# Attention outputs as features by queries, two heads to a product, divided by spread reciprocals

## The chip, the cores and the metric

The kernel runs on one core of one Trainium2 chip. TensorE multiplies, VectorE and ScalarE work on elements, GpSimd does a few small things, and SyncE issues the transfers; each works through its own list of instructions in order and waits on semaphores for the others. The metric is the time of one execution on the device in microseconds, as the median of several runs.

## The reference

A trunk of two layers, each a half-step SwiGLU block, a token mixer and another half-step SwiGLU block, on 256 tokens of 1024 features. Every sub-layer is entered through an RMS norm with an adaLN scale and shift and left through an adaLN gate, which are products of the conditioning vector with weights. The first layer's mixer is multi-head latent attention, the second's a Mamba-2 scan (SSD). The change is in the attention, whose core is:

```
def one_block(args):                       # a block of 128 queries, 2 of them
    q_blk, i = args
    s = jnp.einsum('bhqd,bhkd->bhqk', q_blk, kt) * scale      # 16 heads of 96
    s = jnp.where(k_pos[None, :] <= q_pos[:, None], s, -jnp.inf)
    p = jax.nn.softmax(s, axis=-1).astype(vt.dtype)
    return jnp.einsum('bhqk,bhkd->bhqd', p, vt)               # values of 64
...
return o.reshape(Bn, S, MLA_HEADS * V_HEAD) @ w_o
```

Everything is float32. The large products are made of three products of two rounded parts each (a high part and a residue, `split_pair`, `split_act`, `mm3`); the scores and the products with the values are plain float32.

## The kernel before

The features lie on the partitions, the 256 tokens on the free axis. `run` goes through six sub-layers; `mla` (from L811) is the second. Weights come in pieces of 1 MB through five buffers; each piece is split by ScalarE (L206, the high part) and VectorE (L207, the residue `wlo`). The adaLN products are done on VectorE in halves of 128x1024 (L237, `ada_half`), which the program calls wherever there seemed to be room, and which any later sub-layer needs.

The attention goes head by head in turns (`turn`, L1075). In turn t the 16 heads stand at different steps: `scores(t)` on TensorE, queries on the partitions; `softmax(t - 1)`, two maxima on VectorE (L1015, L1016) and two exponentials on ScalarE (L1020), which also leave the sum of a row in `den`; `probs_t(t - 2)`, three transposes of the probabilities; `probs_evac(t - 3)`, their copy to SBUF, by VectorE for three heads of four; `values(t - 4)`. There the transposed probabilities are the stationary side and the 64 columns of a head's values stream, so that a bank holds four heads (a quad) as queries by features. For each quad `o_evac` takes reciprocals of `den` and multiplies (L1053, L1055), `o_t` transposes the result back to features by queries with four transposes, and `o_split` splits it for the output projection. Between the turns the projections of the next quads' queries run. The last turns are hooks of `down`, between products of the output projection (`mwo`).

The order on each engine is not that of the code: the framework's scheduler sets it when the program is built, from priorities and costs of its own, and only instructions that are pinned (`keep_in_program_order`) keep their place. The adaLN halves, the weight splits and the attention are not pinned, so an edit of one moves the others.

A product that resembles the new one is in the SSD scan (`ymm`, L1304): a stationary of 64 columns for each of two heads, into the two halves of the partitions of a bank.

Of the kernel before, what the change touches and what calls it, by code (L numbers as in the profile page):

```python
# [8 lines left out]
F32R = mybir.dt.float32r  # L9
# [3 lines left out]
ALU = mybir.AluOpType  # L13
# [51 lines left out]
class Trunk:  # L65
# [745 lines left out]
    def mla(self, s):  # L811
# [182 lines left out]
        SC, PB, PTs, O, DEN, OT, ON, OB = {}, {}, {}, {}, {}, [], {}, {}  # L994
# [29 lines left out]
        def probs_t(h):  # L1024
            P = SC.pop(h)
            pp = PB[h] = self.bank()
            for b in range(3):
                self.transpose(out=pp[:, b * 128:(b + 1) * 128], in_=P[:, b * 128:(b + 1) * 128],
                                    identity=self.ident)
# [8 lines left out]
        def values(h):  # L1038
            quad, hh = divmod(h, 4)
            half, h8 = divmod(h, 8)  # L1040
            if hh == 0:
                O[quad] = self.bank()
            PT = PTs.pop(h)
            hc = slice(h8 * 64, (h8 + 1) * 64)
            o0 = O[quad][:, hh * 64:(hh + 1) * 64]
            o1 = O[quad][:, 256 + hh * 64:256 + (hh + 1) * 64]
            self.matmul(o1, PT[:, 0:128], V[0][half][:, hc], start=True, stop=False)
            self.matmul(o1, PT[:, 128:256], V[1][half][:, hc], start=False, stop=True)
            self.matmul(o0, PT[:, 256:384], V[0][half][:, hc], start=True, stop=True)

        def o_evac(quad):
            den = DEN.pop(quad)
            nc.vector.reciprocal(out=den, in_=den)  # L1053
            t = ON[quad] = self.slot()
            nc.vector.tensor_tensor(  # L1055
                out=t.rearrange("p (c h d) -> p c h d", c=2, d=64),
                in0=O.pop(quad).rearrange("p (c h d) -> p c h d", c=2, d=64),
                in1=den.rearrange("p c (h o) -> p c h o", o=1).broadcast_to([128, 2, 4, 64]), op=ALU.mult)

        def o_t(quad):  # L1060
            t = ON.pop(quad)
            ps = OB[quad] = self.bank()
            for b in range(2):
                for c in range(2):
                    self.transpose(out=ps[:, b * 256 + c * 128:b * 256 + (c + 1) * 128],
                                        in_=t[:, c * 256 + b * 128:c * 256 + (b + 1) * 128], identity=self.ident)
# [559 lines left out]
```

## Time and profile before

| | |
|---|---|
| median of 3 runs | 1079.45 us (1079.35 to 1080.08) |
| the profiled execution | 1078.63 us |
| its span | 1076.9 us |
| TensorE busy | 1060.8 us, 98% |
| VectorE busy | 872.2 us, 81% |
| ScalarE busy | 617.8 us, 57% |
| chain that ended last | TensorE 92%, DMA 4%, VectorE 3%, ScalarE 1% |

Times of rows are microseconds from the start of the span. PE is TensorE's matmul, DVE is VectorE, ACT is ScalarE. A float32 matmul leaves two records in the trace. Records on one engine overlap a little, since each reaches from its start to its last result: the time that one takes from the engine is the distance to the start of the next, and not its length.

### The profile page before, as it was taken

To read this page: it belongs to the slowest core of one execution; us is meant where nothing else is said; L and a number is where in the kernel's file an instruction comes from. 1 tells how busy PE (TensorE), PEld (TensorE's weight loads), DVE (VectorE), ACT (ScalarE), POOL (GpSimd) and SP (SyncE) were. 2 spreads that over 40 slices of the span, in tenths; PEclk is the share of its full clock that TensorE was granted. 3 is DMA by queue.
4 is the path that set the end of the run, shared out by engine and by line. 5 is a ranking of instruction groups with operands and counts; after the bars stand their busy time and mean duration, and the time that the engine had idled before them with its cause. 6 is when DMAs were issued, how large, how long until landed. Compare 5 with 4: busy or idle time off the path is not lost.

```text
span 1076.9 us, 21729 instructions
## 1 busy us (share of the span) xinstructions
PE 1060.8 (98%) x8814; PEld 1044.1 (97%) x8814; DVE 872.2 (81%) x1551; ACT 617.8 (57%) x1099; POOL 41.3 (4%) x102
## 2 busy tenths in 40 slices
PE   7999999999999999999999999999999999999998
PEld 5999999999999999999999999999999899999998
DVE  5899988889989977767999886599999688756642
ACT  5564544479567444444754544498899567544431
POOL 0000000000010000100000000000211000000000
PEclk9999999999999999999999999999999999999999
DMA  9999998854366988765699987544344354666630
GB/s 353 337 368 342 337 360 321 291 197 148 109 229 221 343 311 312 283 232 202 246 365 346 335 319 250 181 165 157 118 137 170 144 194 161 251 214 214 229 128 21
DMA packets 38264, 259.59 MB, mean 241 GB/s; under 512 B 4370, under 2 KB 5522, under 8 KB 8084
## 3 DMA queue, kind: packets, MB, share of 16 engines
q1 hardware_dynamic: 38164, 258.21, 65.9%
q8 instruction: 69, 1.13, 0.4%
q14 instruction: 31, 0.25, 0.1%
HBM read 257.14 MB, written 1.05 MB: 240 GB/s over the span
## 4 chain that ended last, share of the span: by engine, by line
PE 92%; DMA 4%; DVE 3%; ACT 1%; issue 0%; SPq 0%; ACTq 0%
PE bank L295 91%; DMA raw<-in_adao_dram 3%; PE bank L300 1%; DVE raw L259 1%; DMA raw<-in_xt_dram 0%; DVE wlo L613 0%; ACT sl L808 0%; ACT t L1020 0%; ACT whi L206 0%; DVE sl L1474 0%; DVE ssq L942 0%; ACT t L937 0%; DVE wlo L207 0%; DVE mx L1015 0%; ACT sl L806 0%
## 5 line engine op out<-in xcount | busy, mean ns | idle before, releaser
L295 PE MATMUL bank<-sl,whi 128*128 128x256 f32 (+2 forms) x5360 | 956.2, 282 | 4.9 <-ACT sl L647 3.6
L295 PEld LDWEIGHTS bank<-sl,whi 128*128 128x128 f32 (+1 forms) x5360 | 818.5, 188 | 8.6 <-ACT sl L647 4.6
L295 PE MATMUL bank<-sl,wlo 128*128 128x256 f32 (+2 forms) x2680 | 746.6, 280 | 0.0
L206 ACT CAST whi<-raw 128x1024 fp32r<-128x1024 f32 (+1 forms) x329 | 341.4, 1041 | 339.6 <-PE bank L295 243.8
L295 PEld LDWEIGHTS bank<-sl,wlo 128*128 128x128 f32 (+1 forms) x2680 | 503.6, 188 | 0.2
L207 DVE TENSOR_TENSOR wlo<-raw,whi 128x1024 fp32r<-128x1024 f32 (+1 forms) x329 | 398.1, 1213 | 105.5 <-ACT whi L206 102.0
L237 DVE SCALAR_TENSOR_TENSOR raw<-raw,cb 128x1024 f32<-128x1024 f32 x128 | 154.4, 1218 | 7.6 <-DMA raw<-in_adaw_dram 7.6
L329 ACT CAST sl<-t 128x256 fp32r<-128x256 f32 x125 | 48.6, 403 | 12.2 <-DVE t L521 7.0
L330 DVE TENSOR_TENSOR sl<-t,sl 128x256 fp32r<-128x256 f32 x125 | 51.1, 418 | 1.0 <-ACT sl L329 0.7
L521 DVE TENSOR_TENSOR t<-t,bank 128x256 f32<-128x256 f32 x70 | 28.7, 416 | 15.6 <-PE bank L295 15.6
L460 DVE SCALAR_TENSOR_TENSOR x<-bank,mod,x 128x256 f32<-128x256 f32 x48 | 22.9, 480 | 22.2 <-PE bank L295 21.8
L1159 DVE SCALAR_TENSOR_TENSOR sl<-t,cst,sl 128x256 f32<-128x256 f32 x72 | 34.7, 490 | 0.2
L410 ACT ACTIVATE sl<-x,scol 128x256 fp32r<-128x256 f32 x40 | 20.3, 508 | 23.8 <-DVE x L460 23.7
L520 ACT ACTIVATE t<-bank 128x256 f32<-128x256 f32 x70 | 25.9, 378 | 0.0
L409 POOL CAST sl<-bspl 128x4 fp32r<-128x4 f32 x40 | 12.7, 364 | 319.4 <-PE bank L295 232.6
L259 DVE SCALAR_TENSOR_TENSOR raw<-raw,cb 128x1024 f32<-128x1024 f32 x16 | 19.5, 1222 | 5.9 <-DMA raw<-in_adao_dram 5.8
L295 PE MATMUL bank<-whi,sl 128*128 128x384 f32 (+1 forms) x80 | 24.3, 368 | 0.0
L440 POOL TENSOR_TENSOR rr<-rv,mhalf 128x2 f32<-128x2 f32 x11 | 11.8, 1071 | 304.3 <-DVE rv L436 304.3
L1297 ACT ACTIVATE dec<-sl,nac 128x128 f32<-128x128 f32 x64 | 20.5, 394 | 4.8 <-DVE sl L1286 4.5
L411 DVE SCALAR_TENSOR_TENSOR sl<-x,scol,sl 128x256 fp32r<-128x256 f32 x40 | 19.2, 480 | 4.2 <-ACT sl L410 4.0
L423 ACT ACTIVATE t<-t,mod,scol 128x256 f32<-128x256 f32 x32 | 18.3, 595 | 3.7 <-DVE t L422 3.6
L613 DVE TENSOR_TENSOR wlo<-raw,whi 128x1024 fp32r<-128x1024 f32 (+1 forms) x17 | 19.5, 1156 | 0.0
(215 smaller groups left out, 650.1 us busy)
## 6 DMA issues: line engine op xcount, KB each, us to landing
raw<-in_wgu_dram SPq DMA_DIRECT2D x80, 1024.0 KB, 5.3
raw<-in_adaw_dram SPq DMA_DIRECT2D x64, 1024.0 KB, 6.1
raw<-in_wdn_dram SPq DMA_DIRECT2D x44, 1024.0 KB, 6.2
raw<-in_win_dram SPq DMA_DIRECT2D x19, 1024.0 KB, 4.9
raw<-in_wout_dram SPq DMA_DIRECT2D x8, 1024.0 KB, 4.9
raw<-in_wop_dram SPq DMA_DIRECT2D x6, 1024.0 KB, 6.1
raw<-in_adao_dram SPq DMA_DIRECT2D x6, 1024.0 KB, 8.1
raw<-in_mwo_dram SPq DMA_DIRECT2D x4, 1024.0 KB, 4.9
```

Source lines behind the costliest of these rows:

```text
L206: self.nc.scalar.copy(out=hi, in_=raw)
L207: self.nc.vector.tensor_tensor(out=lo, in0=raw, in1=hi.bitcast(F32), op=ALU.subtract)
L237: nc.vector.scalar_tensor_tensor(out=w, in0=w, scalar=1.0, in1=self.cb, op0=ALU.mult, op1=ALU.mult, accum_out=self.mod[:, q, 2 * u + i:2 * ...
L259: self.order(nc.vector.scalar_tensor_tensor(out=w, in0=w, scalar=1.0, in1=self.cb, op0=ALU.mult, op1=ALU.mult, accum_out=self.mod[:, q, c]))
L295: ins = self.nc.tensor.matmul(*a, **k)
L329: self.nc.scalar.copy(out=hi, in_=src)
L330: self.nc.vector.tensor_tensor(out=lo, in0=src, in1=hi.bitcast(F32), op=ALU.subtract)
L460: nc.vector.scalar_tensor_tensor(out=self.x[m], in0=ps[:, 0:T], scalar=self.mod[:, q, m:m + 1], in1=self.x[m], op0=ALU.mult, op1=ALU.add)
L520: nc.scalar.activation(out=tg, in_=pg[:, 0:T], func=AF.Silu)
L521: nc.vector.tensor_tensor(out=tg, in0=tg, in1=pu[:, 0:T], op=ALU.mult)
L1159: nc.vector.scalar_tensor_tensor(out=dst, in0=u[:, t:t + T], scalar=cw[:, t:t + 1], in1=dst, op0=ALU.mult, op1=ALU.add)
L1297: self.order(nc.scalar.activation(out=t[:, j, 2 * c], in_=q[:, o:o + 128], func=AF.Exp, bias=self.nac[:, c, h:h + 1]))
```

## The change

The products with the values change sides: the values of a head, 64 columns, are the stationary, and the transposed probabilities stream. Two heads (a pair) share a bank, one in each half of the partitions, and the result is features by queries at once. `o_t` goes, and `values` is called for a pair in every second turn. The division now needs each reciprocal on 64 partitions, as a row over the queries: `divisors` takes the reciprocals of a quad's `den` on VectorE and spreads them by eight products with the identity, whose stationary is a column of `den` broadcast to 64; `rows` copies that bank to SBUF on ScalarE; `o_evac` multiplies a pair. The attention needs two turns fewer.

```diff
@@ -991,7 +991,7 @@
         QT[0] = [self.heads_evac(b, None) for b in qb]
         q_evac(1, 1, p1)
 
-        SC, PB, PTs, O, DEN, OT, ON, OB = {}, {}, {}, {}, {}, [], {}, {}
+        SC, PB, PTs, O, DEN, OT, ON, DB = {}, {}, {}, {}, {}, [], {}, {}
 
         def scores(h):
             quad, hh = divmod(h, 4)
@@ -1022,11 +1022,12 @@
             SC[h] = P
 
         def probs_t(h):
+
             P = SC.pop(h)
             pp = PB[h] = self.bank()
             for b in range(3):
-                self.transpose(out=pp[:, b * 128:(b + 1) * 128], in_=P[:, b * 128:(b + 1) * 128],
-                                    identity=self.ident)
+                o = (b + 1) % 3 * 128
+                self.transpose(out=pp[:, o:o + 128], in_=P[:, b * 128:(b + 1) * 128], identity=self.ident)
 
         def probs_evac(h):
             PTs[h] = self.t3()
@@ -1035,42 +1036,47 @@
             else:
                 nc.vector.tensor_copy(out=PTs[h], in_=PB.pop(h)[:, 0:384])
 
-        def values(h):
...
+        def values(pair):
+
+            ps = O[pair] = self.bank()
+            hs = [2 * pair, 2 * pair + 1]
+            PT = [PTs.pop(h) for h in hs]
+            for c in range(2):
+                for j, h in enumerate(hs):
+                    half, h8 = divmod(h, 8)
+                    self.matmul(ps[j * 64:(j + 1) * 64, c * 128:T], V[c][half][:, h8 * 64:(h8 + 1) * 64],
+                                PT[j][:, c * 256:256 + c * 128], start=(c == 0), stop=(c == 1))
+        def divisors(quad):
+
             den = DEN.pop(quad)
             nc.vector.reciprocal(out=den, in_=den)
-        def o_t(quad):
...
+            ps = DB[quad] = self.bank()
+            for i in range(2):
                 for c in range(2):
-        def o_split(quad):
...
+                    for j in range(2):
+                        h = 2 * i + j
+                        self.matmul(ps[j * 64:(j + 1) * 64, i * T + c * 128:i * T + (c + 1) * 128],
+                                    den[:, c, h:h + 1].broadcast_to([128, 64]), self.ident, start=True, stop=True)
+
+        def rows(quad):
+            t = DB[quad]
+            DB[quad] = self.slot()
+            nc.scalar.copy(out=DB[quad], in_=t)
+
+        def o_evac(pair):
+            quad, i = divmod(pair, 2)
+            ps = O.pop(pair)
+            if i == 0:
+                ON[quad] = self.slot()
+            nc.vector.tensor_tensor(out=ON[quad][:, i * T:(i + 1) * T], in0=ps[:, 0:T], 
+                                    in1=DB[quad][:, i * T:(i + 1) * T], op=ALU.mult)
+            if quad == 3:
+                OT.append(self.split_act(ON[quad][:, i * T:(i + 1) * T]))
+            elif i:
+                hi, lo = self.slot(F32R), self.slot(F32R)
+                self.split_pair(hi, lo, ON.pop(quad))
+                for b in range(2):
+                    OT.append((hi[:, b * T:(b + 1) * T], lo[:, b * T:(b + 1) * T]))
 
         def turn(t):
 
@@ -1086,10 +1092,12 @@
                 probs_evac(t - 3)
             if 0 <= t - 1 < HEADS:
                 softmax(t - 1)
-            if t >= 8 and t % 4 == 0:
-                o_evac(t // 4 - 2)
-            if t >= 10 and t % 4 == 2:
-                o_split(t // 4 - 2)
+            if t >= 5 and t % 4 == 1:
+                divisors(t // 4 - 1)
+            if t >= 6 and t % 4 == 2:
+                rows(t // 4 - 1)
+            if t >= 6 and t % 2 == 0:
+                o_evac(t // 2 - 3)
             if t < HEADS:
                 scores(t)
             if nq < 4:
@@ -1102,24 +1110,22 @@
                     q_rstd(nq)
             if 0 <= t - 2 < HEADS:
                 probs_t(t - 2)
-            if 0 <= t - 4 < HEADS:
-                values(t - 4)
-            if t >= 9 and t % 4 == 1:
-                o_t(t // 4 - 2)
+            if t >= 5 and t % 2 == 1:
+                values(t // 2 - 2)
             if quad + 1 < 4:
                 if hh == 1:
                     turn.qb = quad_t(QQ[quad + 1])
                 if hh == 2:
                     QT[quad + 1] = [self.heads_evac(b, None) for b in turn.qb]
 
-        tail = HEADS + 3
+        tail = HEADS + 1
         for t in range(tail):
             turn(t)
 
         def last(t):
             turn(t)
             self.ada_half(2)
-        rest = [lambda t=t: last(t) for t in range(tail, HEADS + 7)]
+        rest = [lambda t=t: last(t) for t in range(tail, HEADS + 5)]
         self.down(s, 8, lambda k: OT[k], rest, 2, 2, 1, MLA_EVERY)
 
 
```

The scheduler's new order differs over the whole attention. Three places follow; in them heads count from 0, quads are heads 0 to 3, 4 to 7 and so on.

On TensorE, at quad 1. `bank_3486` before and `bank_3499` now take the transposes of head 6, `bank_3504` and `bank_3523` the scores of head 9, `bank_3490` the values of quad 1. Before:

```order
L300 MATMUL bank_3486<-ident,t_570_3444 128x128 x2
L295 MATMUL bank_3490<-sl_2944,t_568_3438 128x64
L295 MATMUL bank_3490<-sl_2946,t_568_3438 128x64
L300 MATMUL bank_3486<-ident,t_570_3444 128x128
L295 MATMUL bank_3490<-sl_2944,t_568_3438 128x64
L295 MATMUL bank_3504<-sl_3141,sl_3434 128x256
L295 MATMUL bank_3504<-sl_3141,sl_3434 128x128
L295 LDWEIGHTS identb
L295 MATMUL bank_3504<-maskq,identb 128x256
```

Now, with the divisors of quad 1 in `bank_3514` and the values of heads 4 and 5 in `bank_3531`:

```order
L300 MATMUL bank_3499<-ident,t_573_3453 128x128 x3
L295 MATMUL bank_3514<-ident,den_3348 64x128 x8
L295 MATMUL bank_3523<-sl_3141,sl_3443 128x256
L295 MATMUL bank_3523<-sl_3141,sl_3443 128x128
L295 LDWEIGHTS identb
L295 MATMUL bank_3523<-maskq,identb 128x256
L300 MATMUL bank_3527<-ident,t_582_3487 128x128 x3
L295 MATMUL bank_3531<-t_571_3447,sl_2944 64x256
L295 MATMUL bank_3531<-t_580_3481,sl_2944 64x256
```

The divisors stand between the transposes of a head and the scores of the next turn, so these scores wait with them for `den_3348`. It is the same at quad 0 (behind the transposes of head 2) and at quad 2 (head 10); at quad 3 twelve products of the output projection stand in between.

On VectorE, at quad 1, from the copy of head 6's probabilities to the reciprocal of the quad. Before:

```order
L1036 COPY t_583_3494<-bank_3486 128x384
L771 TENSOR_TENSOR rst_3454<-rsy_3453 128x2x4
L1015 TENSOR_REDUCE mx_3497<-bank_3482 128x1
L772 TENSOR_TENSOR rst_3454<-rst_3454,ssq_3364 128x2x4
L1016 TENSOR_REDUCE mx_3497<-bank_3482 128x1
L773 TENSOR_SCALAR rst_3454<-rst_3454 128x2x4
L1015 TENSOR_REDUCE mx_3532<-bank_3504 128x1
L774 TENSOR_TENSOR rsy_3453<-rsy_3453,rst_3454 128x2x4
L1017 SCALAR_TENSOR_TENSOR mx_3497<-mx_3497,cq_3307 128x2
L1016 TENSOR_REDUCE mx_3532<-bank_3504 128x1
L952 TENSOR_TENSOR cq_3461<-rsy_3453,rqs_2905 128x8
L1053 RECIPROCAL den_3352<-den_3352 128x8
```

Now, where `raw_2978` and `raw_3190` are adaLN weights and `sl_3492` is the residue of quad 0's output:

```order
L1037 COPY t_587_3503<-bank_3499 128x384
L773 TENSOR_SCALAR rst_3463<-rst_3463 128x2x4
L1017 SCALAR_TENSOR_TENSOR mx_3506<-mx_3506,cq_3307 128x2
L237 SCALAR_TENSOR_TENSOR raw_2978,mod<-raw_2978,cb 128x1024
L774 TENSOR_TENSOR rsy_3462<-rsy_3462,rst_3463 128x2x4
L207 TENSOR_TENSOR sl_3492<-sl_3422,sl_3491 128x512
L952 TENSOR_TENSOR cq_3470<-rsy_3462,rqs_2905 128x8
L1052 RECIPROCAL den_3348<-den_3348 128x8
L237 SCALAR_TENSOR_TENSOR raw_2978,mod<-raw_2978,cb 128x1024
L237 SCALAR_TENSOR_TENSOR raw_3190,mod<-raw_3190,cb 128x1024
L1015 TENSOR_REDUCE mx_3548<-bank_3523 128x1
```

An adaLN half and a residue of 128x512 have come between the copy and the reciprocal, and two halves behind it, ahead of the next maximum; the maxima that stood there are elsewhere. Of the six adaLN halves of this stretch three stood ahead of the last copy of probabilities before, and all six do now, with one more weight residue (three instead of two).

On VectorE, at the reciprocal of quad 0, as a piece of the difference between the two orders (`mx_3405` is the maximum of head 5, `raw_2962` adaLN weights; directly ahead of the piece stands, in both, the copy from `bank_3342`, the transposes of head 2):

```order
 L772 TENSOR_TENSOR rst_3300<-rst_3300,ssq_3222 128x2x4
-L1017 SCALAR_TENSOR_TENSOR mx_3353<-mx_3353,cq_3184 128x2
-L1015 TENSOR_REDUCE mx_3405<-bank_3360 128x1
+L1017 SCALAR_TENSOR_TENSOR mx_3349<-mx_3349,cq_3184 128x2
+L1052 RECIPROCAL den_3210<-den_3210 128x8
 L773 TENSOR_SCALAR rst_3300<-rst_3300 128x2x4
-L1016 TENSOR_REDUCE mx_3405<-bank_3360 128x1
+L237 SCALAR_TENSOR_TENSOR raw_2962,mod<-raw_2962,cb 128x1024
 L774 TENSOR_TENSOR rsy_3299<-rsy_3299,rst_3300 128x2x4
-L1053 RECIPROCAL den_3210<-den_3210 128x8
+L237 SCALAR_TENSOR_TENSOR raw_2962,mod<-raw_2962,cb 128x1024
 L952 TENSOR_TENSOR cq_3307<-rsy_3299,rqs_2905 128x8
```

The reciprocal has moved ahead by a few places, and two adaLN halves have taken the place of the maximum of head 5.

On VectorE, at quad 2, now (`bank_3611` is the transposes of head 10, `raw_3317` weights of the output projection, `sl_3604` the residue of quad 1's output):

```order
L207 TENSOR_TENSOR wlo_3832<-raw_3317,whi_3831 128x1024
L1037 COPY t_619_3615<-bank_3611 128x384
L1015 TENSOR_REDUCE mx_3618<-bank_3607 128x1
L1016 TENSOR_REDUCE mx_3618<-bank_3607 128x1
L207 TENSOR_TENSOR sl_3604<-sl_3557,sl_3603 128x512
L1017 SCALAR_TENSOR_TENSOR mx_3618<-mx_3618,cq_3470 128x2
L1052 RECIPROCAL den_3505<-den_3505 128x8
```

The weight residue ahead of the copy and the residue of quad 1's output were not in this place before.

## Rows read from the trace of the kernel before

**Rows 1.** The page: busy time, share of the span and instructions of each engine.

```profile
PE 1060.8 (98%) x8814; PEld 1044.1 (97%) x8814; DVE 872.2 (81%) x1551; ACT 617.8 (57%) x1099; POOL 41.3 (4%) x102
```

**Rows 2.** Busy time of each engine by windows, the attention and what follows.

```profile
core 0: us, PE busy (x) PEld busy (x) DVE busy (x) ACT busy (x) POOL busy (x), PEclk, DMA share, GB/s
...
260.00:270.00 10.00, 9.78 (x76) 9.20 (x76) 8.74 (x33) 9.01 (x29) 0.00 (x0) 1.00 0.32 107
270.00:280.00 10.00, 10.00 (x83) 9.63 (x84) 9.40 (x34) 7.97 (x28) 0.00 (x0) 1.00 0.01 2
280.00:290.00 10.00, 9.62 (x85) 9.25 (x84) 9.28 (x25) 5.50 (x19) 1.00 (x10) 1.00 0.29 105
290.00:300.00 10.00, 10.00 (x87) 10.00 (x86) 9.75 (x19) 5.17 (x9) 3.29 (x8) 1.00 0.76 274
300.00:310.00 10.00, 10.00 (x87) 10.00 (x87) 9.63 (x18) 6.83 (x12) 0.00 (x0) 1.00 0.70 252
```

**Rows 3.** Waits of TensorE, 230 to 300 us: total, times, longest.

```profile
PE bank L300 <- ACT t L1020: 1.0, 2, 0.6
PE bank L295 <- DVE t L1036: 0.2, 1, 0.2
```

**Rows 4.** TensorE's timeline in the attention: start, length, instruction, count.

```profile
274.82 0.78 PE L295 MATMUL bank<-sl,t 128*128 128x64 f32 x6
275.44 0.87 PE L295 MATMUL bank<-sl,sl 96*128 96x256 f32 x4
276.15 0.28 PE L295 MATMUL bank<-maskq,identb 128*128 128x256 bf16 x1
...
280.64 0.61 PE L300 MATMUL bank<-ident,sl 128*128 128x128 f32 x4
281.08 0.82 PE L295 MATMUL bank<-sl,sl 96*128 96x256 f32 x4
281.74 0.27 PE L295 MATMUL bank<-maskq,identb 128*128 128x256 bf16 x1
```

**Rows 5.** TensorE's timeline at a product of the SSD scan.

```profile
747.14 0.40 PE L295 MATMUL bank<-sl,whi 128*128 128x256 f32 x2
747.38 0.28 PE L295 MATMUL bank<-sl,wlo 128*128 128x256 f32 x1
747.59 0.87 PE L295 MATMUL bank<-dec,sl 128*64 128x256 f32 x8
748.39 0.50 PE L295 MATMUL bank<-acr,s_pick 128*128 128x256 f32 x2
748.73 0.40 PE L295 MATMUL bank<-sl,whi 128*128 128x256 f32 x2
```

**Rows 6.** VectorE's timeline at the first reciprocal.

```profile
262.52 0.19 DVE L1053 RECIPROCAL den<-den 128x8 f32<-128x8 f32 x1
```

**Rows 7.** VectorE's timeline, an adaLN half and what follows it.

```profile
279.50 1.22 DVE L237 SCALAR_TENSOR_TENSOR raw<-raw,cb 128x1024 f32<-128x1024 f32 x1
...
280.64 0.55 DVE L1036 COPY t<-bank 128x384 f32<-128x384 f32 x1
281.11 0.41 DVE L1015 TENSOR_REDUCE mx<-bank 128x1 f32<-128x256 f32 x1
281.44 0.28 DVE L1016 TENSOR_REDUCE mx<-bank 128x1 f32<-128x128 f32 x1
281.90 0.69 DVE L207 TENSOR_TENSOR sl<-bank,sl 128x512 fp32r<-128x512 f32 x1 [0.18 <-ACT sl L206]
282.51 0.15 DVE L1017 SCALAR_TENSOR_TENSOR mx<-mx,cq 128x2 f32<-128x2 f32 x1
```

**Rows 8.** TensorE's timeline at the transposes of head 2.

```profile
259.86 0.44 PE L300 MATMUL bank<-ident,t 128*128 128x128 f32 x2 [0.64 <-ACT t L1020]
```

**Rows 9.** ScalarE's timeline, the last exponential of quad 0.

```profile
261.59 0.21 ACT L1020 ACTIVATION_READ_ACCUMULATOR t<-bank,mx,cq 128x1 f32 x1
```

**Rows 10.** The page's costliest groups: a multiplication from a bank, 128x256.

```profile
L521 DVE TENSOR_TENSOR t<-t,bank 128x256 f32<-128x256 f32 x70 | 28.7, 416 | 15.6 <-PE bank L295 15.6
```

More of the change, by code (lines that the diff above doesn't have):

```diff
@@ L1036, in probs_evac @@
                 nc.vector.tensor_copy(out=PTs[h], in_=PB.pop(h)[:, 0:384])
-        def values(h):
[L1039 to L1049, printed above, removed]
@@ L1051, in o_evac @@
-        def o_evac(quad):
+        def values(pair):
[7 more added lines that the diff above has]
+                                PT[j][:, c * 256:256 + c * 128], start=(c == 0), stop=(c == 1))
@@ L1052, in o_evac @@
+        def divisors(quad):
             den = DEN.pop(quad)
             nc.vector.reciprocal(out=den, in_=den)
[L1054 to L1058, printed above, removed]
-        def o_t(quad):
-            t = ON.pop(quad)
-            ps = OB[quad] = self.bank()
-            for b in range(2):
-                for c in range(2):
-                    self.transpose(out=ps[:, b * 256 + c * 128:b * 256 + (c + 1) * 128],
-                                        in_=t[:, c * 256 + b * 128:c * 256 + (b + 1) * 128], identity=self.ident)
@@ L1068, in o_split @@
-        def o_split(quad):
-            ps = OB.pop(quad)
-            hi, lo = self.slot(F32R), self.slot(F32R)
-            self.split_pair(hi, lo, ps)
-            for b in range(2):
-                OT.append((hi[:, b * T:(b + 1) * T], lo[:, b * T:(b + 1) * T]))
+            ps = DB[quad] = self.bank()
+            for i in range(2):
+                for c in range(2):
+                    for j in range(2):
+                        h = 2 * i + j
+                        self.matmul(ps[j * 64:(j + 1) * 64, i * T + c * 128:i * T + (c + 1) * 128],
+                                    den[:, c, h:h + 1].broadcast_to([128, 64]), self.ident, start=True, stop=True)
```

## The prediction

> **What bounds the kernel now.** First the busy times of the engines: TensorE is busy for 98% of the span [rows 1]; nearly every microsecond of it is a microsecond of the result. The attention stretch, from about 250 to 290 us, is where the change lies. In the windows of 10 us from 260 to 300 TensorE is busy for 9.6 to 10.0, but VectorE for 8.7 to 9.8 as well [rows 2]: two engines close to full, that hand each head to and fro. The waits of TensorE there come to 1.2 us, 1.0 for a softmax of ScalarE and 0.2 for a copy of VectorE [rows 3]. Behind it, from 290 us on, TensorE runs without a gap (10.00 of 10.00) [rows 2], so what is lost in the attention is not won back.
>
> So two questions decide: what the change does to TensorE's own work, and whether it puts a new wait of TensorE on VectorE.
>
> **TensorE's own work.** The products with the values took six records a head, 274.82 to 275.44 us, 0.62 us, and the scores behind them began late by some 0.05 (0.71 against 0.66 us to the mask) [rows 4]: 0.67 x 16 = 10.7 us. The four transposes of each quad's output, 280.64 to 281.08, are 0.44 x 4 = 1.8 us [rows 4]. Both go.
>
> The new product has the shape of one that this kernel has: the scan of the SSD layer puts 64 columns of stationary into each half of the array, streams 256 and then 128 float32 columns, and writes the halves of the partitions in turn. Eight records from 747.59 to 748.39 us: 0.80 us, for what would be 1.3 us one after the other by the scores' pace (a head's 384 columns in 0.66 us [rows 4]): the halves run side by side. Before it stands a gap of 0.09 (747.38 and a pitch of 0.12 make 747.50), and the two records behind it take 0.34 instead of 0.24 [rows 5]. So 0.99 us a pair, 8 pairs, 7.9 us: a gain of 2.8.
>
> The divisors add, for each quad, eight float32 products of 128 columns, 16 records. Side by side they are 8 steps of 0.11 (a third of the 384 columns in 0.66 us, in two records each), 0.88, and with the same edges of about 0.25, 1.15; four quads, 4.6 us. No row shows a column broadcast as a stationary of 64; if the halves do not overlap it is 4 x 2.0 = 8.0, and it cannot be under the 8 steps, 3.5. I take 4.6, by the scan. The sum is 4.6 - 2.8 - 1.8 = 0.0 us.
>
> The edges of 0.25 a group are 12 x 0.25 = 3.0 of this. The Trainium skill, page TensorEngine Tiling (Array Packing), section Key Properties, says that a change of the tiling mode, unlike a change of tile, drains TensorE; the scan's gap before and slow start behind agree with it. Its section Performance Considerations advises just this swap for a moving side of 64 columns, with up to twice the speed; halving the values would gain 5.3 us where the scan's rows give 2.8.
>
> **The new wait.** A quad's divisors need its reciprocal, and this is what they cost. Before, nothing on TensorE waited for a reciprocal; the output was divided on VectorE a turn or two later. Now TensorE has the divisors right behind a head's transposes and ahead of the next scores (the pieces of the order in the section on the change). TensorE works in order, so scores, projections and transposes stand still until VectorE has come to the reciprocal.
>
> Quad 1. The transposes of head 6 are directly ahead of the divisors, and VectorE's copy of these very transposes is ahead of the reciprocal. Whatever the state of the engines, the wait is thus at least VectorE's list from the copy on: copy 0.47, a small one 0.15, a half of an adaLN product 1.14, the residue of 128x512 0.61, reciprocal 0.19 [rows 6, 7], and three operations of 128x8 of about 0.1 between: 2.8 us. The adaLN half and the residue were not there before.
>
> Quad 2. Here from the copy: copy 0.47, the two maxima 0.33 and 0.28, residue 0.61, 0.15 and 0.19: 2.0 us if VectorE stood ready at the copy; ahead of the copy stands a weight residue of the adaLN half's size, and if that has just begun 1.1 more: 3.2. VectorE is behind by then (next part), so I take the middle and not the floor, 2.5.
>
> Quad 0. TensorE's transposes of head 2 end at 260.2 (259.86 and three of 0.11) [rows 4, 8]. ScalarE ends the last exponential of the quad at 261.59 + 0.21 = 261.80 [rows 9]; the reciprocal (0.19) and a hop put the divisors at 262.05: 1.85 us. The floor is 0.8 (copy, small one, reciprocal), the ceiling 2.5, if the reciprocal comes when the old one did, 262.52 + 0.19 [rows 6].
>
> Quad 3. Twelve products of the output projection, 0.12 each, stand between the last transposes and the divisors, and the reciprocal is right behind the copy: no wait, at most 0.7.
>
> **What VectorE gets besides.** In the new order all six adaLN halves of the stretch and one more weight residue stand before the last copy of the probabilities; before it were three halves. That is 4 x 1.14 = 4.6 us, and the eight multiplications of 128x256 at about 0.34 (0.42 less the overlap [rows 10]) for four of 0.61, with two small ones, add 0.6 over the whole. VectorE had 27.4 of 30 us from 260 to 290 [rows 2]; it now has 32. This alone says that the stretch grows by at least 2 us, whatever TensorE does. It also makes the maxima of heads 5 and 6 late, behind the two halves after the first reciprocal: I put 0.4 us for one late softmax (0 to 0.9 by the waits seen [rows 3]). Of the 1.2 us of old waits the first, 0.64, is ahead of the divisors and stays; the others vanish in the new ones: -0.6.
>
> ScalarE copies the divisors, four times 128x512; with two turns fewer at the end these cost nothing, as long as ScalarE's slack (5.5 to 9.0 us busy of 10 [rows 2]) covers them; else half a microsecond each, 2 us. The last turns come two earlier, but TensorE had no gap there, so this is worth nothing.
>
> **Sum.** 1.85 + 2.8 + 2.5 + 0.4 - 0.6 + 0.0 = 7.0 us. The profiled execution took 1078.63 us (a span of 1076.9 and 1.7 around it): 1085.6. The median of the runs is 0.8 above it, 1079.45: 1086.4.
>
> **Rivals.**
> - No change: VectorE does early what it would have done late, and the waits are given back. For it: the adaLN halves have to be done anyway. Against it: after 290 us TensorE waits for nothing [rows 2], so a VectorE that has less to do there releases nobody. 1079.5; chance 0.08.
> - Faster: VectorE gets to each reciprocal before TensorE gets to the divisors. It needs a TensorE that is late by more than 2.8 us at quad 1, and by the common copy it cannot be. If it were, the gain is the tile work: at the best -2.8 - 1.8 + 3.5 = -1.1 with all old waits gone, -2.3: 1077.1. Chance 0.05. The page's halving, 2.5 us more, would make it 1074.6; the scan's rows are against it.
> - Slower still: divisors one after the other, since all eight stream the same identity: 8.0 instead of 4.6, 1089.8. Against it is the scan, though there both halves stream different columns. Chance 0.07.
> - The waits at their floors (0.8 + 2.8 + 2.0, all old waits gone, edges smaller): +3 to +4, 1082.9. Chance 0.10.
> - That the change does not do what it says: the pieces of the order show the divisors' products and their place; I give this nothing.
>
> **How the numbers follow.** The forecast has 0.70; its own range is 1083.5 to 1089.5. For the whole I reach down to the floors and up to the serial divisors, 1082 to 1089.8. Slower by over 0.2% (2.2 us, about what a measurement of this kernel can tell from no change) are the forecast, the floors and the serial case: 0.87; same 0.08; faster 0.05.
>
> **What would show it.** In the new profile the waits of TensorE between 250 and 300 us should rise from 1.2 to some 8 us, named for VectorE's reciprocal, in three pieces: about 1.9, 2.8 and 2.5. Each pair's eight records should take 0.8 us, the divisors' 16 about 0.9. VectorE should show its two adaLN halves in a row behind the first reciprocal. I am wrong if the waits at the divisors are under 1 us, or if TensorE shows gaps after 300 us that were not there; and wrong on the size if the divisors' pairs start 0.1 us apart and not together.

## The result

The changed kernel takes 1094.58 us (median of 5 runs, 1092.86 to 1097.43), the kernel before 1079.45 us (5 runs, 1077.52 to 1080.46). The ratio is 1.0141, 95% interval 1.0127 to 1.0155: slower by 15.1 us, where 7 were forecast and 10.3 was the upper end of the range. The sign was right, the size was not.

The profile after has a span of 1092.8 us, 15.9 more than before. TensorE's row of the page, to be read against [rows 1], hardly differs, and misleads: 8.9 us more of "busy".

```profile
PE 1069.7 (98%) x8830; PEld 1046.3 (96%) x8830; DVE 872.5 (80%) x1556; ACT 620.9 (57%) x1104; POOL 37.3 (3%) x102
```

The windows of the attention, in the columns of [rows 2]:

```profile
260.00:270.00 10.00, 7.98 (x53) 6.46 (x53) 8.15 (x29) 7.06 (x21) 0.00 (x0) 0.83 0.34 107
270.00:280.00 10.00, 6.61 (x50) 5.07 (x48) 9.59 (x31) 6.65 (x24) 0.00 (x0) 0.85 0.31 106
280.00:290.00 10.00, 9.35 (x60) 7.07 (x56) 7.02 (x21) 5.07 (x17) 0.00 (x0) 0.81 0.56 210
290.00:300.00 10.00, 8.15 (x71) 6.73 (x71) 6.13 (x21) 5.82 (x21) 0.47 (x5) 1.00 0.01 2
```

Two things have changed against [rows 2]. TensorE is busy for 6.6 to 8.2 us of 10 in the windows from 260, 270 and 290 us, where it was for 9.8 to 10.0. And the column of the granted clock, 1.00 throughout before, stands at 0.83, 0.85 and 0.81 in three windows. The window from 280 to 290 us shows why busy time alone does not do: it is 9.35 busy, nearly the old 9.62, but holds 60 matmuls where the old one held 85.

TensorE's waits from 230 to 320 us (total, times, longest), against [rows 3]:

```profile
PE bank L295 <- DVE den L1052: 2.9, 1, 2.9
PE bank L295 <- DVE bspl L281: 2.3, 1, 2.3
PE bank L295 <- DVE rst L773: 1.5, 1, 1.5
PE bank L300 <- ACT t L1020: 1.4, 3, 0.6
```

They sum to 8.1 us, 6.9 more than before. The three for VectorE are those of the divisors of quads 1, 2 and 0; they carry the name of what ended last, and only one of them that of the reciprocal (`den`). TensorE's timeline shows them in their places, and what follows them:

```profile
262.79 1.47 PE L295 MATMUL bank<-ident,den 128*64 128x128 f32 x16 [1.47 <-DVE rst L773]
264.19 1.65 PE L295 MATMUL bank<-sl,sl 96*128 96x256 f32 x4
...
268.28 0.87 PE L295 MATMUL bank<-t,sl 128*64 128x256 f32 x8
...
278.27 1.98 PE L295 MATMUL bank<-ident,den 128*64 128x128 f32 x16 [2.87 <-DVE den L1052]
280.18 1.65 PE L295 MATMUL bank<-sl,sl 96*128 96x256 f32 x4
...
282.61 1.45 PE L295 MATMUL bank<-t,sl 128*64 128x256 f32 x8
...
291.64 1.09 PE L295 MATMUL bank<-ident,den 128*64 128x128 f32 x16 [2.30 <-DVE bspl L281]
...
300.26 1.09 PE L295 MATMUL bank<-ident,den 128*64 128x128 f32 x16
```

The same four score products that took 0.82 us in [rows 4] take 1.65 behind the first two waits; sixteen divisor records take 1.98 us at 278.27 and 1.09 at 291.64; a pair's eight value records take 1.45 at 282.61 and 0.87 at 268.28. Durations doubled at one place and normal at another are a clock and not a dependency. Record by record the granted clock is 0.5 (1.2 GHz instead of 2.4) from 263.4 to 266.8 and from 277.0 to 283.8 us, 1.0 elsewhere in the stretch. In the first 3.4 us TensorE worked throughout, of the second it worked from 278.3 on, 5.6 us. Half of 3.4 + 5.6 is 4.5 us: that is the estimate of what the clock cost.

So the attention's account is 6.9 us of waits and 4.5 of clock, 11.4 together, in this execution. How long the clock stands at 0.5 differs from one execution to the next: the mean granted clock of the five runs is 0.992 to 0.997 (0.995 in the profiled one), and the run at 0.992 is the longest, the one at 0.997 the shortest. Measured by VectorE's residual additions (line 460), the last one ahead of the attention starts 1.2 us later than before, the first one behind it 12.7: the attention grew by 11.5. The other 3.2 us come later, without a wait of TensorE: by the last addition of each layer 0.6 in the first feed-forward layer behind the attention, 1.1 in the second, -0.3 in the SSD layer, 1.8 in the last.

### The profile page after: what moved, and what is told of

Same layout as the page of the kernel before. It is cut to its first block, busy times and chain, and to the rows that moved or that the text cites. A ratio compares the mean times of both kernels' runs of the same rounds, so it can differ in the third digit from the quotient of the medians.

```text
span 1092.8 us, 21772 instructions
## 1 busy us (share of the span) xinstructions
PE 1069.7 (98%) x8830; PEld 1046.3 (96%) x8830; DVE 872.5 (80%) x1556; ACT 620.9 (57%) x1104; POOL 37.3 (3%) x102
## 4 chain that ended last, share of the span: by engine, by line
PE 91%; DMA 4%; DVE 3%; ACT 1%; issue 0%; SPq 0%; ACTq 0%
PE bank L295 90%; DMA raw<-in_adao_dram 3%; DVE raw L259 1%; PE bank L300 1%; ACT t L1020 0%; DMA raw<-in_xt_dram 0%; DVE wlo L613 0%; ACT sl L808 0%; DVE wlo L207 0%; DVE t L1037 0%; DVE mx L1015 0%; ACT whi L206 0%; DVE ssq L942 0%; DVE sl L1480 0%; ACT t L937 0%
## 5 line engine op out<-in xcount | busy, mean ns | idle before, releaser
L207 DVE TENSOR_TENSOR wlo<-raw,whi 128x1024 fp32r<-128x1024 f32 (+1 forms) x329 | 398.2, 1215 | 95.4 <-ACT whi L206 93.8
L409 POOL CAST sl<-bspl 128x4 fp32r<-128x4 f32 x40 | 9.6, 290 | 315.4 <-PE bank L295 234.5
L1020 ACT ACTIVATE t<-bank,mx,cq 128x256 f32<-128x256 f32 (+1 forms) x32 | 16.2, 514 | 6.2 <-DVE mx L1017 5.8
```

The source lines that it names most:

```text
L207: self.nc.vector.tensor_tensor(out=lo, in0=raw, in1=hi.bitcast(F32), op=ALU.subtract)
```

## The experiments

All were compared with the kernel before on the same chip in the same rounds; before had medians of 1079.5 to 1080.2 us there.

| Run | What it changes | us | ratio, 95% interval |
|---|---|---|---|
| e1 | divisors from a column of ones | 1086.31 | 1.0052 (1.0034 to 1.0070) |
| e2 | filler products in place of the waits | 1087.99 | 1.0083 (1.0052 to 1.0115) |
| e3 | no division at all | 1079.85 | 1.0001 (0.9992 to 1.0011) |
| e4 | adaLN halves held back | 1088.58 | 1.0084 (1.0066 to 1.0102) |
| e5 | as e3, value products together | 1076.70 | 0.9970 (0.9959 to 0.9981) |
| e6 | whole change, divisors later | 1081.78 | 1.0019 (1.0010 to 1.0028) |
| e8 | division on GpSimd | 1088.33 | 1.0079 (1.0066 to 1.0092) |
| e9 | before, four more buffers | 1080.98 | 1.0008 (0.9999 to 1.0016) |
| e10 | as e8, a turn later | 1083.34 | 1.0030 (1.0020 to 1.0039) |
| e11 | before, one wait added | 1084.74 | 1.0048 (1.0036 to 1.0061) |
| e12 | as e10, shared with ScalarE | 1081.02 | 1.0005 (0.9996 to 1.0014) |

**e1: no wait for the reciprocals.** The divisors' products take a column of ones as stationary, so that they are made but need nothing of VectorE.

```
-  den[:, c, h:h + 1].broadcast_to([128, 64]), self.ident, ...
+  self.ones[:, h:h + 1].broadcast_to([128, 64]), self.ident, ...
```

> The divisors' products take a column of a constant tile of ones as their stationary instead of the column of reciprocals, so the division is left out of the result; every product, copy and multiplication of the change is still done, and the reciprocals too, but nobody waits for them. Theory: the change lost 15 us because TensorE stands at the divisors for VectorE's reciprocals (about 8 us in three waits) and then runs at half its clock for some 3.4 and 6.8 us; its own products cost what before's cost. So without the wait no clock falls, the three waits go, and the time is 1079 to 1081. First rival: the products with 64 columns of stationary and the switches between them and the full array are dear by themselves; then 1088 or more stays. Second rival, for the 3 us that the changed kernel lost behind the attention, where TensorE never waited: if that comes from other buffers being used there, it stays, and the time is 1082 to 1084 with a granted clock of 1.0.

1086.31 us: 8 us of the 15 gone, but not all; the time lies outside the ranges of the theory and of both rivals. Its only wait of TensorE from 230 to 320 us is

```profile
PE bank L300 <- ACT t L1020: 0.6, 1, 0.6
```

and the clock stayed at 1.0. Of the 7.7 us by which its span is longer than that of before, 2.9 lie ahead of the attention, 2.5 in it and 2.2 behind. The 2.5 are not the price of the change's own products where these stand together: taking the wait away had also moved the order. In 3 of the 8 pairs a transpose now stood between the value products, and in 3 of the 4 quads one between the divisors' products. They took 8.1 and 5.2 us in all, 3.1 more than in e6, where nothing stands between them (see e3 and e5).

**e2: work in place of idleness.** Ahead of the divisors of quads 0, 1 and 2 stand 2, 3 and 2 products of 512 float32 columns that nobody needs; the code is otherwise that of the changed kernel.

```
+  self.pin = True
+  for _ in range((2, 3, 2, 0)[quad]):
+      self.matmul(ps, self.ident, self.cb[:, 0:512], start=True, stop=True)
+  self.pin = False
```

> The changed kernel with 2, 3 and 2 extra float32 products of 512 columns (about 0.86 us each) ahead of the divisors of quads 0, 1 and 2, written to the divisors' own bank and overwritten by them: TensorE works where it stood still. The waits for the reciprocals stay as they are. Theory: 4 to 5 of the 15 us are work done at half clock behind the waits (263.4 to 266.8 us, and from 278.3 to 283.8, at half speed). So the granted clock stays at 1.0 and the time falls to about 1090, with a little lost again where the extra work is longer than the wait (up to 0.7 us at quad 0). Rival: the clock's fall costs nothing, since VectorE would have held TensorE up by as much; then 1094 to 1096.

1087.99 us: 6.6 us faster than the changed kernel, with more work in it, and 2 less than the theory's 1090. TensorE is kept from its other work nearly as long as before (the seven fillers take 6.0 us, the three waits took 6.6), but it is busy meanwhile. The order moved a little as well: the next scores now stand between the fillers and the divisors.

```profile
261.92 1.88 PE L295 MATMUL bank<-cb,ident 128*128 128x512 f32 x4
264.39 1.09 PE L295 MATMUL bank<-ident,den 128*64 128x128 f32 x16
...
274.43 2.74 PE L295 MATMUL bank<-cb,ident 128*128 128x512 f32 x6
277.01 0.82 PE L295 MATMUL bank<-sl,sl 96*128 96x256 f32 x4
...
277.87 1.09 PE L295 MATMUL bank<-ident,den 128*64 128x128 f32 x16
```

```profile
270.00:280.00 10.00, 9.53 (x67) 6.23 (x65) 9.13 (x33) 6.46 (x24) 0.00 (x0) 1.00 0.35 115
280.00:290.00 10.00, 9.84 (x74) 7.04 (x68) 9.04 (x29) 6.21 (x21) 0.00 (x0) 1.00 0.54 205
```

The divisors take 1.09 us everywhere, the clock is 1.00. No wait for VectorE is left. This separates the two parts of the loss: the 6 us that TensorE is kept from its work remain, whether it idles or not; the doubled durations go with the idleness. Added up by the starts of its records, waits and fillers left out, TensorE's work of the attention between the residual additions takes 91.54 us in the changed kernel and 87.15 here: 4.4 us, where the estimate had 4.5. The rest of the 6.6 us lies behind the attention.

**e3 and e5: no division.** e3 leaves out the reciprocals, their products, ScalarE's copies and the division; e5 does that too and pins the four value products of a pair next to each other.

```
 # e3: division out                     # e5: e3, and in values()
-  divisors(t // 4 - 1)                 +  self.pin = True
+  DEN.pop(t // 4 - 1)                     for c in range(2): ...
-  rows(t // 4 - 1)                     +  self.pin = False
```

> The values stationary for two heads as in the change, but no reciprocals, no divisors and no copies of them: each pair is copied from its bank without being divided, so the division is left out of the result. Theory: this is the gain of the swapped products alone, 2.8 us for the products and 1.8 for the four output transposes of each quad, so 1074 to 1076, or 1077 to 1079 if the 3 us behind the attention stay; against the run with ones it shows the price of the divisors' products, 4 to 5 us. Rival: the swapped products are no gain inside the attention, because VectorE paces it; then no less than 1079.

> The undivided kernel again (reciprocals, their products, their copies and the division left out), with the four value products of a pair kept next to each other on TensorE. In the undivided run a transpose stood between the two 256-column products of 7 of the 8 pairs and the value products took 10.4 us. Theory that the broken neighbourhood ate the gain: value products about 6.7 us (as in the run with filler products, where they stood together), so some 3.7 us less, 1076 to 1078, faster than before. Rival, that the gain of two heads side by side is lost elsewhere (the transposes that follow, the evictions): 1079 to 1080, the same as before.

e3 came out even with before, 1079.85 us, although it does less, as its rival had it. Its timeline shows the reason at a pair:

```profile
269.25 0.65 PE L295 MATMUL bank<-t,sl 128*64 128x256 f32 x2
269.83 0.33 PE L300 MATMUL bank<-ident,t 128*128 128x128 f32 x1
270.09 0.87 PE L295 MATMUL bank<-t,sl 128*64 128x256 f32 x6
270.88 0.92 PE L295 MATMUL bank<-sl,sl 96*128 96x256 f32 x4
```

With a transpose between the two heads' first products the first one runs alone: 1.63 us from 269.25 to 270.88, of which the transpose is 0.26. In e5 the same eight records stand together:

```profile
268.29 0.87 PE L295 MATMUL bank<-t,sl 128*64 128x256 f32 x8
```

and the kernel takes 1076.70 us, 3.3 less than before and in the range of e5's theory; so it was not VectorE's pace, e3's rival, that had held e3 up. Added up over the attention the value products take 10.4 us in e3 and 6.4 in e5; before they were 9.6 and the outputs' transposes 1.7. So the swap is a gain as long as nothing stands between the two heads: 3.3 us, where the forecast's terms had 2.8 + 1.8 = 4.6. By the records the value products and the transposes give 4.9 us, and TensorE's other work of the stretch, with the edges of these products in it, takes 1.4 more than before. The Trainium skill, page TensorEngine Tiling (Array Packing), section Key Properties, has both halves of this: tiles work in parallel, and a change of the tiling mode drains TensorE. The rows agree: one transpose of the whole array in the middle makes the pair 0.83 us longer, its own 0.26 and 0.57 of overlap.

**e4: VectorE's list.** The six adaLN halves of the stretch are pinned in their place in VectorE's queue, behind the work of the attention that was written ahead of them.

```
-  nc.vector.scalar_tensor_tensor(out=w, in0=w, ...)
+  ins = nc.vector.scalar_tensor_tensor(out=w, in0=w, ...)
+  if self.hold:
+      self.order(ins)
```

> The changed kernel with the six adaLN halves of this stretch kept in VectorE's order behind everything of the attention. The divisors and their waits on the reciprocals stay, with the reciprocal of quad 1 four short operations behind the copy instead of behind an adaLN half and a residue. Theory: the halves that slipped into the attention make the waits long; quad 0 stays at 1.9 us, quad 1 falls from 3.3 to about 1, quad 2 from 2.5 to about 1, and with them most of the fall of the clock: 1084 to 1087. Rival: the reciprocals are late because of the exponentials and of TensorE's own order, whatever VectorE does beside them; then 1091 or more.

1088.58 us, 6 less than the changed kernel, but above the 1084 to 1087 of the theory. The waits for VectorE at the divisors become 3.9 us in all (the kernel's lines are 4 further down):

```profile
263.20 1.09 PE L299 MATMUL bank<-ident,den 128*64 128x128 f32 x16 [1.47 <-DVE rst L777]
...
275.32 1.41 PE L299 MATMUL bank<-ident,den 128*64 128x128 f32 x16 [1.37 <-DVE den L1056]
...
286.44 1.09 PE L299 MATMUL bank<-ident,den 128*64 128x128 f32 x16 [1.08 <-DVE mx L1021]
```

and there is one stretch at half clock (276.0 to 279.4 us), behind the second wait, instead of two. The first wait is as long as in the changed kernel, at the same place, and this time the clock stays at 1.00 behind it. The halves are thus part of the waits, but not the whole of them: with the divisors ahead of the scores, TensorE waits for whatever VectorE has in its queue.

**e6: the whole change, divisors later in the turn.** The reciprocal stays where it was; its products go behind the transposes and value products of the turn. The value products are pinned as in e5, and the divisors' products of a quad too.

```
-  (in divisors, at the start of the turn: the eight products)
+  if t >= 5 and t % 4 == 1:
+      spread_div(t // 4 - 1)        # behind probs_t and values
```

> The whole change, dividing included, but the products with the reciprocals stand at the end of their turn, behind the transposes and the value products, instead of at its start. Nothing else is moved. Theory (three waits for VectorE plus the halved clock that follows them make nearly all of the loss): the waits for the reciprocals shrink to under 1 us in sum, the clock stays at full speed, the attention is 1 to 2 us longer than before, 1081 to 1084. Rival, that TensorE's own work for the change costs 3 us or more whatever the waits are: 1086 to 1088, as with the column of ones.

1081.78 us, within the 1081 to 1084 of the theory: 12.8 of the 15.1 us are gone, with every operation of the change still there. All of its waits of TensorE, and its windows:

```profile
PE bank L300 <- ACT t L1020: 0.8, 2, 0.6
PE bank L295 <- DVE sl L207: 0.4, 1, 0.4
```

```profile
260.00:270.00 10.00, 9.37 (x77) 8.13 (x75) 9.23 (x36) 9.67 (x29) 0.00 (x0) 1.00 0.39 142
270.00:280.00 10.00, 9.87 (x83) 7.73 (x83) 9.89 (x36) 8.37 (x29) 0.00 (x0) 1.00 0.04 12
280.00:290.00 10.00, 9.72 (x84) 7.81 (x84) 9.30 (x29) 7.78 (x27) 0.58 (x6) 1.00 0.29 105
```

The waits are back at 1.2 us, the sum of [rows 3], the clock at 1.00. The order of VectorE followed, without being asked: the adaLN half that stood ahead of the second reciprocal now stands behind it. So e6 does not tell the two moves apart; it shows that the place of the products decides about both. It is still 2 us (1.1 to 3.0) slower than before. By the residual additions that is not lost in the attention, which takes 0.5 us less than before in the profile: 3.0 us lie ahead of it and 1.4 behind.

**e11: one wait, and nothing else.** The kernel before, with a maximum over 3 x 1024 columns on VectorE in one turn; its result is not used.

```
+  if t == 5:
+      self.order(nc.vector.reduce_max(out=junk, in_=<cb, three times>, axis=AX.X))
```

> The kernel before with one added instruction: a maximum over 3 x 1024 columns on VectorE (some 3.2 us by the row of the 256-column maximum, 0.42 us, whose result is not used), ahead of the copy of probabilities in the turn that follows the first quad. It makes TensorE wait once and changes nothing else. Theory that a wait of 2 to 3 us brings the halved clock for some us behind it, as in the changed kernel: the granted clock falls to 0.5 once for 3 to 6 us and the kernel loses the wait (1.5 to 2.5 us) and 1.5 to 3 us more, 1083 to 1085. Rival, that the clock falls only where several waits follow each other: the clock stays at 1.0 and the kernel loses the wait alone, 1081 to 1082.5.

1084.74 us, 5.2 more than before and within the theory's 1083 to 1085. The added instruction took 3.35 us from 261.3 us on; TensorE felt it 10 us later, through a softmax:

```profile
271.12 0.28 PE L295 MATMUL bank<-maskq,identb 128*128 128x256 bf16 x1
273.60 0.44 PE L300 MATMUL bank<-ident,t 128*128 128x128 f32 x2 [2.21 <-ACT t L1020]
...
275.09 1.59 PE L295 MATMUL bank<-sl,sl 96*128 96x256 f32 x4
...
280.88 0.82 PE L295 MATMUL bank<-sl,sl 96*128 96x256 f32 x4
```

```profile
270.00:275.00 5.00, 2.79 (x20) 2.41 (x20) 4.47 (x19) 2.72 (x11) 0.00 (x0) 0.90 0.00 0
275.00:280.00 5.00, 5.00 (x24) 4.72 (x24) 3.21 (x13) 2.29 (x11) 0.00 (x0) 0.50 0.01 2
280.00:285.00 5.00, 5.00 (x38) 4.78 (x37) 3.29 (x9) 2.70 (x9) 0.00 (x0) 0.92 0.64 213
```

The whole window from 275 to 280 us is at 0.50 and "busy" for 5.00, with 24 matmuls in it. Record by record the half clock lasts from 273.95 to 280.78 us, 6.8 us, and costs 3.4, more than the wait of 2.2 itself. The attention grew by 5.7 us, which is the two together. All five runs of e11 have a mean clock under 1 (0.995 to 0.998), the runs of before beside them 0.999 or 1.000. So the fall of the clock is not a matter of the divisors or of several long waits: one wait of this length, in a kernel whose other work is unchanged, is enough.

**e9: looking for the later 3 us.** TensorE is busy without a break in both kernels in these stretches, and yet there are fewer matmuls in the same time. Windows in two later feed-forward layers (columns: TensorE's busy time and instructions, granted clock, DMA share, GB/s), before:

```profile
540.00:600.00 60.00, 60.00 (x514) 1.00 0.94 353
960.00:1010.00 50.00, 50.00 (x427) 1.00 0.59 211
```

after:

```profile
540.00:600.00 60.00, 60.00 (x508) 1.00 0.88 329
960.00:1010.00 50.00, 50.00 (x420) 1.00 0.56 201
```

The changed kernel takes 16 buffers of the shared ring of 30 in the attention instead of 12, so that all later tiles lie elsewhere. e9 takes 16 in the kernel before.

```
   t = ON[quad] = self.slot()
+  nc.gpsimd.memset(self.slot()[:, 0:3], 0.0)
```

> The kernel before with four more 512-column buffers taken from the shared ring inside the attention (each written in three columns by GpSimd and never read), so that the ring stands where it stands in the changed kernel (16 buffers taken there instead of 12). Theory that the 3 us which the changed kernel loses behind the attention come from the ring's position: 1081 to 1083, and the mean distance of matmuls in the third and fourth feed-forward layers rises from 117.3 and 118.0 ns to 118.3 and 119.8 ns. Rival, that it comes from later work or transfers that the slower attention displaced: 1079 to 1080, distances as before.

1080.98 us: 1.0 more than before, interval -0.1 to 1.7. In the two windows it has 510 and 427 instructions, so the first layer is slower and the second is not. And e6, which takes 16 buffers as well, has 512 and 425. The ring's place can't be the whole of it; what slows these matmuls by some 1.2 and 1.6% stays open. Each count is from one execution, and none of the kernels here has more than before; they reach from 507 to 514 and from 419 to 427 (e11, with before's buffers, has 513 and 424): how much of it is scatter between executions can't be told.

**e8, e10, e12: looking for a version that beats both.** e5 shows 3.3 us to be had if the division costs TensorE nothing. These three divide the probabilities, while the queries are still on the partitions, by GpSimd, which is 4% busy [rows 1]. e10 has one turn more between exponential and transpose, e12 gives four of the last heads to ScalarE.

```
+  nc.vector.reciprocal(out=rec, in_=den[:, :, hh])
+  for c, sl in ((1, slice(0, 256)), (0, slice(256, 384))):
+      nc.gpsimd.tensor_scalar(out=P[:, sl], in0=P[:, sl], scalar1=rec[:, c:c + 1], ...)
   # e12: for h in (9, 11, 13, 15) nc.scalar.activation(..., func=AF.Copy, scale=rec[:, c:c + 1])
```

> A version meant to beat both: values two heads at a time as in the change, but the division is made on the probabilities by GpSimd before their transposes (two multiplications of 128x256 and 128x128 for a head, the reciprocals of a head on VectorE), one turn later for all that follows; no products with reciprocals and no copies of rows. Theory (TensorE is the bound and is spared 10.4 + 1.7 - 6.7 us of work at best, less the waits): 1076 to 1079. Rival, that GpSimd's two multiplications and their hand-over (about 1.0 us for 128x256 by the row of GpSimd's 128x256 additions, so 1.6 us and more for a head) make the transposes late: TensorE waits a few tenths of a us in most of 16 turns, 1082 to 1086.

> The division by GpSimd on the probabilities again, with the transposes and all that follows them one more turn later, so that GpSimd's two multiplications (1.12 and 0.70 us in the first such run, which made TensorE wait 5.4 us in 7 waits) have a turn of 2.6 us more. Theory that the hand-over's lateness is the whole loss: no waits for GpSimd, full clock, value products side by side in all 8 pairs, 1076 to 1079, faster than before or the same. Rival, that the longer pipeline takes buffers that others wait for (10 tiles of 384 columns, 8 banks) or that GpSimd slows VectorE: 1081 to 1085.

> The division on the probabilities, one turn later as in the second such run, with the multiplications of heads 9, 11, 13 and 15 on ScalarE instead of GpSimd, since GpSimd was busy without a pause from 273.3 to 283.9 us there (1.78 us for a head against turns of about 1.75 us in the last quad) and TensorE then waited 2.2 and 1.3 us and ran at half clock for 3.4 us. Theory that these last two waits and the clock behind them are the remaining loss: no wait over 1 us, full clock, some 5 us less than 1083.3, so 1077 to 1080, the same as before or a little faster. Rival, that ScalarE, which also makes the exponentials, becomes late itself: 1081 to 1084.

e8 (1088.33) came out above the range of its rival, e10 (1083.34) in that of its rival, but the reason was not the one given there: in both GpSimd's hand-over was late, as e8's rival had it. In e10 GpSimd (first line) had no pause for 12 multiplications, 1.78 us a head, and TensorE waited at the end of that, with 3.4 us at half clock behind the wait:

```profile
273.27 10.65 POOL L1058 TENSOR_SCALAR t<-t,rec 128x256 f32<-128x256 f32 x12 [0.55 <-DVE mx L1017]
```

```profile
286.46 1.05 PE L300 MATMUL bank<-ident,t 128*128 128x128 f32 x3 [2.16 <-POOL t L1058]
```

e12 has no wait above 0.74 us and a clock of 1.00 throughout, and takes 1081.02 us, at the lower end of its rival's range and not to be told from before. Its waits of TensorE still sum to 3.4 us, 2.2 more than before, of the 3.3 that e5 had to give. No version here beats the kernel before.

## Why the prediction was right in sign and wrong in size

**Right: the waits.** Forecast were 1.85, 2.8 and 2.5 us at the divisors of quads 0, 1 and 2 and none at quad 3; the rows above say 1.47, 2.87, 2.30 and none. VectorE's list in the changed kernel is the one the forecast added up, the two adaLN halves behind the first reciprocal included:

```profile
262.53 0.20 DVE L1052 RECIPROCAL den<-den 128x8 f32<-128x8 f32 x1
...
262.68 1.22 DVE L237 SCALAR_TENSOR_TENSOR raw<-raw,cb 128x1024 f32<-128x1024 f32 x1
...
275.51 0.55 DVE L1037 COPY t<-bank 128x384 f32<-128x384 f32 x1
...
276.12 1.22 DVE L237 SCALAR_TENSOR_TENSOR raw<-raw,cb 128x1024 f32<-128x1024 f32 x1
...
277.34 0.68 DVE L207 TENSOR_TENSOR sl<-sl,sl 128x512 fp32r<-128x512 f32 x1
...
278.02 0.20 DVE L1052 RECIPROCAL den<-den 128x8 f32<-128x8 f32 x1
```

The late softmax, 0.4, is there too (1.4 for 1.0 in the waits on line 1020), and the 0.2 on line 1036 is gone. All waits together: 6.9 us more, where the sum had 6.95. In this two errors cancel: the waits at the divisors are 0.5 shorter than forecast, and of the old waits only those 0.2 vanished and not 0.6.

**Right: TensorE's own work, at full clock.** The sum put 0.0. The attention's 11.5 us less 6.9 of waits and 4.5 of clock leave 0.1. By parts, from e6, where the clock is whole: values 6.2 us and divisors 4.0, without their edges (forecast with edges: 7.9 and 4.6). The halves overlap, also where all eight products stream the identity, so the rival of serial divisors is out. The old products were 9.6 us by their starts, where the forecast had 10.7 with the late scores behind them; the errors of the terms, each under 2 us, cancel. Not right is the forecast's side argument that VectorE's list alone makes the stretch at least 2 us longer, whatever TensorE does: in e6 VectorE has the same operations, with five of the six adaLN halves ahead of the last copy of probabilities, and the attention is no longer than before.

**Wrong: the step "1.85 + 2.8 + 2.5 + 0.4 - 0.6 + 0.0 = 7.0".** It prices each wait at its length, and the work behind it at the durations of the rows of before, all of which were taken at a granted clock of 1.00. It has no term for what a wait does to the work behind it. That term is 4.5 us (1.7 behind quad 0, 2.8 behind quad 1). e2 shows that it goes when TensorE is kept busy through nearly the same delay, e11 that a wait of 2.2 us alone brings 3.4 us of it, e6 that it goes with the waits. The column with the clock stood in [rows 2] and was read as a constant. The Trainium skill, page TensorE: Matmul & The Clock Gate, section HAM oscillation, describes TensorE falling back to 1.2 GHz when waits for DMA break up its work; the runs here show the same fall behind waits on VectorE and ScalarE, of 1.37 us (e4), 1.47, 2.21 (e11) and 2.87.

It is not each wait that does it: quad 2's 2.30 us has no half clock behind it, quad 0's 1.47 has, and the same 1.47 at the same place in e4 has not. So the length alone does not decide, and the 4.5 us belong to the profiled execution: the five runs' mean clocks, 0.992 to 0.997, say by estimate ((1 - clock) x span, idle time included) 3 to 9 us. What tells the waits apart was not tried.

**Missing and open: 3.2 us behind the attention.** The forecast said that TensorE runs there without gaps and loses nothing more. There are no gaps, but its matmuls stand further apart. e9 makes the ring's place an unlikely cause of more than about 1 us of it; the cause was not found. Scatter is a rival that was not ruled out: from the last addition of the attention to the end, the changed kernel's profile is 3.0 us longer than before's, and those of the eleven other kernels by -0.2 to 4.1.

**The lead over before in the first 206 us** (1.2 us in the profile) is scatter between executions, as far as can be told: the other kernels, which have the same instructions in the same order up to there, have 0.4 to 3.0.

## What to carry to other kernels

Price a new wait of TensorE as its length plus half of the time that the granted clock then stands at 0.5; here single waits of 1.4 to 2.9 us brought between nothing and 3.4 us more. Where a product needs a result from a busy engine, put it behind work that TensorE has anyway, in the same turn: e6 does the same operations as the changed kernel in 12.8 us less. Products that are to run side by side on parts of the array have to be kept together in the order: here a single full-width transpose between them cost 0.83 us a pair (e3).

## What the hardware showed that was not expected

- One wait of 2.21 us was followed by 6.8 us at half clock in e11, one of 2.30 in the changed kernel by none. A busy TensorE in a window says nothing as long as the clock beside it is not read: 5.00 of 5.00 busy with 24 matmuls against 38 in the next window, itself at 0.92.
- Two heads' 64-column products in the two halves of the array overlap when they are neighbours: a pair takes 1.63 us with a transpose of 0.26 between them, 0.80 without (e3, e5).
- A column broadcast to 64 columns as stationary, with the identity streamed against both halves, overlaps as well: 16 records in 1.03 us (300.26 to 301.29 us in the changed kernel).
- GpSimd's multiplication of a head's probabilities took 1.5 us at its fastest and 2.4 us in other turns (4.80 us for two heads in a row in e10), so that it could not keep pace with the last quad's turns.
